# Token-major products for the convolution inputs of a one-layer hybrid decoder trunk, and later steps in every block-transpose turning

## The chip, the cores and the metric

The kernel runs on one core of one Trainium2 chip. The metric is the device time of one execution in microseconds (us). The core has five engines that run side by side and meet through semaphores: PE (TensorE, matrix products, with weight loads shown apart as PEld), DVE (VectorE), ACT (ScalarE), POOL (GpSimd) and SP (SyncE, which here only issues DMAs). ACT issues DMAs as well, out of the same in-order list as its arithmetic.

## The reference, cut to what matters

One layer with 256 tokens and a model width of 2048. The normed input is multiplied by one wide weight, whose columns are shared out among several branches:

```
proj = h @ w_in
(sb_q, sb_k, sb_v, sb_z, ssd_z, ssd_xbc, ssd_dt, mem_q, mem_z, gate_pre) = split(proj)
o_sb = stick_breaking_attention(sb_q, sb_k, sb_v) * silu(sb_z)          # 8 heads of 128
xbc  = silu(causal_depthwise_conv(ssd_xbc, conv_w, conv_b))             # 4096 channels, 4 taps
x_ssm, b_in, c_in = split(xbc)                                          # 2048, 1024, 1024
y    = ssd_chunked_scan(x_ssm, dt, a, b_in, c_in) + d_skip * x_ssm      # 8 groups of 4 heads
o_ssd = gated_group_rms_norm(y, ssd_z, ssd_norm_w)
o_mem = memory_cross_attention(mem_q, mem_n, w_mem_kv) * silu(mem_z)    # 4 heads of 256
g_sb, g_ssd, g_mem = split(sigmoid(gate_pre + b_gate))
merged = g_sb*(o_sb @ w_branch_sb) + g_ssd*(o_ssd @ w_branch_ssd) + g_mem*(o_mem @ w_branch_mem)
out = rms_norm(x + merged @ w_out, final_norm_w)
```

The change concerns `ssd_xbc`, the 4096 columns that go through the convolution along the tokens.

## The kernel before, in words

All products run on PE in a split float32 form. A weight piece of 512 KB arrives in `raw` (DMA issued by SP, 4 buffers), ACT copies it into a rounded high part `wh` (L146), DVE subtracts to get the low part `wl` (L150), 3 buffers each. The activations `hT` are held the same way, as high and low parts with the model dimension on the partitions.

There are two ways to multiply. `gemm` (L269 to L271) is token-major: 128 tokens of `hT` are the stationary operand and 512 weight columns stream past; for each of 16 k-tiles and both token halves it makes three products of 512 columns (high with high, high with low, low with high). A weight piece holds 2 k-tiles of 512 columns, so it feeds 12 products, and a product over the whole depth takes 8 pieces. `gemm_cols` (L229, L233) is channel-major: 128 weight columns are stationary, and high and low part of `hT` (2 x 256 columns) stream past, then the high part alone (256 columns) against the low weight. A piece there holds 4 k-tiles of 256 columns and feeds 8 products of 512 and 8 of 256 columns. Only the convolution uses `gemm_cols`: 8 groups of 512 channels, two calls each, 4 pieces a call, so 64 pieces in all, as many as 8 calls of `gemm` have.

The convolution needs channels on the partitions. `gemm_cols` delivers that at once: `fold` (L246 on ACT, L247 on DVE) adds the two halves of the accumulator into `cu`, and `taps` (L744, L747) makes four DVE operations for each tile of 128 channels, 32 tiles in all. Other products that need channels on the partitions use `turning`: DVE transposes 32 x 32 blocks out of the accumulator (L308), ACT issues a DMA that writes them to a scratch in DRAM (L313), later four DMAs that read them back in turned order (L322), and later still the result is used.

The order of the work is set by hand. Every weight piece ends with `pump()`, which advances a clock by one, runs what `defer(fn, n)` has put n pieces ahead, and advances one of two lanes of head-by-head work (memory heads, stick-breaking heads, then SSD groups). Everything is written into each engine's in-order list at that moment. Between the copy of one weight piece and that of the next, ACT therefore does whatever was due at that piece; a `wh` copy that comes late makes `wl` late on DVE and then the products late on PE.

After the convolution come the products of the merge gates and the branches. There each gate group has a sigmoid (L772), each SSD group exponentials of its decays `dec` (L812); these need different ACT tables, and a table load (ACT_TABLE_LOAD, L768 or L772) stands where they alternate. DVE adds a mask to the decays (L805), scales the inputs `xs` (L799), weighs the decays (L816) and adds the gate bias into `sig` (L907).

SiLU of the turned gate tiles `zT` and of the convolved tiles `cT` is done by `silu` (L203), four tiles at once. It is issued during the last four convolution groups and shortly after.

Of the kernel before, what the change touches and what calls it, by code (L numbers as in the profile page):

```python
# [10 lines left out]
F32 = mybir.dt.float32  # L11
F32R = mybir.dt.float32r
AF = mybir.ActivationFunctionType
# [3 lines left out]
P = 128  # L17
D = 2048
T = 256
NKT = D // P  # L20
GW = 512
# [4 lines left out]
LATE = 3  # L26
# [10 lines left out]
C_SSDZ, C_XBC, C_DT = 4096, 6144, 10240  # L37
# [4 lines left out]
def trunk_kernel(  # L42
# [6 lines left out]
    nc = tc.nc  # L49
# [4 lines left out]
    tmp = ctx.enter_context(tc.tile_pool(name="tmp", bufs=2))  # L54
# [7 lines left out]
    def nm(s):  # L62
        cnt[0] += 1
        return f"{s}_{cnt[0]}"
# [104 lines left out]
    late = []  # L169
    now = [0]  # L170

    def defer(fn, chunks=LATE):

        cnt[0] += 1
        heapq.heappush(late, (now[0] + chunks, cnt[0], fn))
# [26 lines left out]
    def silu(a, chunks=LATE):  # L202
        defer(lambda: nc.scalar.activation(a, a, AF.Silu), chunks)  # L203
# [35 lines left out]
    def fold(dst, acc):  # L239

        if isinstance(acc, list):
            for b in range(2):
                nc.scalar.activation(dst[:, b], acc[b][:, 1], AF.Copy)
                nc.vector.tensor_tensor(dst[:, b], acc[b][:, 0], dst[:, b], ALU.add)
        else:
            nc.scalar.activation(dst, acc[:, :, 1], AF.Copy)  # L246
            nc.vector.tensor_tensor(dst, acc[:, :, 0], dst, ALU.add)  # L247
# [53 lines left out]
    def turning(use=None, dst=None):  # L301

        scratch = dram.tile([2, P, 4, 4, 32], F32, name=nm("scratch"))

        def evac(rows):
            blocks = tmp.tile([P, 2, 4, 4, 32], F32, tag="blocks", name=nm("blocks"), bufs=1)
            for t in range(2):
                nc.vector.transpose(blocks[:, t].rearrange("p j k c -> p k j c"),  # L308
                                    rows[t].rearrange("p (k j c) -> p k j c", k=4, j=4))
            defer(lambda: away(blocks), 1)  # L310

        def away(blocks):
            nc.scalar.dma_start(scratch.rearrange("t p j k c -> p t (j k c)"),  # L313
                                blocks.rearrange("p t j k c -> p t (j k c)"))
            defer(back, 2)

        def back():
            cols = dst
            if dst is None:
                cols = tmp.tile([P, 8, P], F32, tag="turned", name=nm("turned"), bufs=1)  # L320
            for j in range(4):
                nc.scalar.dma_start(  # L322
                    cols[32 * j:32 * j + 32],
                    scratch[:, :, j].rearrange("t (i r) k c -> r (t i) (k c)", r=32))
            if use is not None:
                defer(lambda: use(cols), 3)
        return evac

    def quarter(a):
# [2 lines left out]
    def tiles(cols, k, n):  # L332
        return cols.rearrange("p i (k c) -> p k i c", c=32)[:, k:k + n]
# [19 lines left out]
    def blocked(a):  # L353
        return a.rearrange("p k (i c) -> p k i c", c=32)
# [47 lines left out]
    hT = Cols(NKT, "hT")  # L402
# [246 lines left out]

    for i, z in enumerate((zM, zS)):  # L650
        for q in range(2):
            silu(z[:, 4 * q:4 * q + 4], LATE + 5 + 2 * i + q)
    defer(start_mem, LATE + 9)

    qS = slot([P, 8, T], F32, "qS")
    kS = slot([P, 8, T], F32, "kS")
# [75 lines left out]

    cT = [slot([P, 8, T], F32, "cT") for _ in range(4)]

    def conv_evac(i0):
        def evac(acc):
            u = tmp.tile([P, 2, T], F32, tag="cu", name=nm("cu"), bufs=2)
            fold(u, acc)
            for b in range(2):
                defer(lambda b=b: taps(u[:, b], i0 + b), 1 + 2 * b)  # L740

        def taps(u, i):
            a = cT[i // 8][:, i % 8]
            nc.vector.tensor_scalar(a, u, convw[:, 3, i:i + 1], convb[:, i:i + 1], ALU.mult,  # L744
                                    ALU.add)
            for s in range(1, 4):
                nc.vector.scalar_tensor_tensor(a[:, s:T], u[:, 0:T - s],  # L747
                                               convw[:, 3 - s, i:i + 1], a[:, s:T],
                                               ALU.mult, ALU.add)
        return evac  # L750

    waiting = [zT[i // 2][:, 4 * (i % 2):4 * (i % 2) + 4] for i in range(4)]
    for i, g in enumerate((4, 5, 6, 7, 0, 1, 2, 3)):
        for j in range(2):
            gemm_cols(hT, NKT, w_in, C_XBC + g * GW + 2 * j * P, conv_evac(4 * g + 2 * j))
        waiting.append(cT[g // 2][:, 4 * (g % 2):4 * (g % 2) + 4])
        if i >= 4:
            for j in range(3):
                silu(waiting.pop(0), 6 if not waiting else 1 + j)


    oD = []
# [6 lines left out]
            tables[0] = True  # L769

    def sigmoid(a):
        nc.scalar.activation(a, a, AF.Sigmoid)  # L772
        tables[0] = False

# [2 lines left out]
    def ssd_group(g):  # L777

        heads = range(4 * g, 4 * g + 4)
        xT = [cT[i // 8][:, i % 8] for i in (2 * g, 2 * g + 1)]  # L780
        zg = turned(zT[g // 4], 2 * (g % 4), 2)

# [85 lines left out]
    def step_apart():  # L868
        yield
# [10 lines left out]

    def start_ssd():

        lanes[1].append(step_apart())
        for i in range(SSD_GROUPS):
            lanes[i % 2].append(ssd_group(i))
        for i in range(SSD_GROUPS):
            lanes[i % 2].append(ssd_cols(i))
# [127 lines left out]
    g = 3  # L1015
# [60 lines left out]
```

## Time and profile before

| what | value |
|---|---|
| median of 3 runs | 1217.72 us (1216.94 to 1218.15) |
| the profiled execution's own time | 1217.57 us |
| its span, first to last instruction | 1215.8 us |
| PE busy | 1204.7 us, 99% |
| DVE busy | 784.7 us, 65% |
| ACT busy | 636.1 us, 52% |
| POOL busy | 49.6 us, 4% |
| granted TensorE clock | 0.998 |
| convolution products, first to last | 469.9 to 658.4 us |
| first gate products and memory branch begin | 658.4 us |

A timeline row gives the start in us, the duration in us, the engine, the line, the operation, output and inputs, the shape and how many were merged into the row; in square brackets stands the idle time of the engine just before, and what ended it. "q" behind an engine's name marks its sequencer, which issues DMAs.

### The profile page before, as it was taken

Reading aid. Unit: us, or ns where it says so; the run is one execution under the profiler, and the core shown is the slowest. Engines: PE = TensorE matmul, PEld = TensorE weight load, DVE = VectorE, ACT = ScalarE, POOL = GpSimd, SP = SyncE. Lnnn points to the kernel's source line nnn. Section 1 sums busy time; section 2 is a strip of 40 time slices with the busy share of each in tenths; the row PEclk is TensorE's granted clock in tenths of the full one; section 3 lists DMA queues with packets and bytes.
Section 4 is the critical chain, followed back from the end, with each engine's and each line's share of the span. In section 5 each row is a group of like instructions: output and inputs, shape, how many; then the busy total and the mean of one; then the engine's idle time right before and its main releaser. Section 6 shows DMA issues by size and latency. Waiting matters only on the chain.

```text
span 1215.8 us, 15596 instructions
## 1 busy us (share of the span) xinstructions
PE 1204.7 (99%) x5852; PEld 1008.3 (83%) x5852; DVE 784.7 (65%) x995; ACT 636.1 (52%) x846; POOL 49.6 (4%) x50
## 2 busy tenths in 40 slices
PE   9999999999999999999999999999999999999997
PEld 7888888888888888888888888888888888888886
DVE  5685664556654555888878758677677755655752
ACT  6754543354445444545665756475756544434541
POOL 0000000000000000010100000000000010110101
PEclk9999999999999999999999999999999999999999
DMA  9978798786776778656567667676865677788751
GB/s 337 338 217 240 206 257 237 245 238 194 205 207 192 214 226 234 176 176 185 175 184 216 213 199 217 186 230 180 238 182 182 208 220 216 228 224 289 254 206 69
DMA packets 168091, 262.56 MB, mean 216 GB/s; under 512 B 11792, under 2 KB 65232, under 8 KB 167888
## 3 DMA queue, kind: packets, MB, share of 16 engines
q1 hardware_dynamic: 135456, 229.51, 62.5%
q10 hardware_dynamic: 32560, 32.06, 9.5%
q8 instruction: 45, 0.74, 0.3%
q14 instruction: 30, 0.25, 0.1%
HBM read 249.45 MB, written 12.09 MB: 215 GB/s over the span
## 4 chain that ended last, share of the span: by engine, by line
PE 93%; DMA 3%; ACT 1%; issue 1%; DVE 1%; ACTq 0%; SPq 0%; POOLq 0%; POOL 0%; DVEq 0%
PE acc L269 24%; PE acc L270 24%; PE acc L271 24%; PE acc L229 10%; PE acc L233 5%; DMA raw<-in_w_mem_kv_dram 1%; PE y L833 1%; DMA turned<-scratch 1%; DMA rows<-in_mem_dram 1%; DVE wl L150 1%; ACT wh L146 1%; PE acc L456 0%; PE acc L457 0%; PE dtp L517 0%; PE acc L1030 0%
## 5 line engine op out<-in xcount | busy, mean ns | idle before, releaser
L150 DVE TENSOR_TENSOR wl<-raw,wh 128x1024 fp32r<-128x1024 f32 (+1 forms) x409 | 502.7, 1233 | 320.0 <-ACT wh L146 318.0
L146 ACT ACTIVATE wh<-raw 128x1024 fp32r<-128x1024 f32 (+1 forms) x409 | 430.9, 1056 | 431.0 <-PE acc L271 311.2
L269 PE MATMUL acc<-wh,hT 128*128 128x512 f32 x896 | 351.5, 392 | 0.0
L270 PE MATMUL acc<-wl,hT 128*128 128x512 f32 x896 | 349.2, 390 | 0.2 <-DVE wl L150 0.2
L271 PE MATMUL acc<-wh,hT 128*128 128x512 f32 x896 | 349.0, 390 | 0.0
L271 PEld LDWEIGHTS acc<-wh,hT 128*128 128x128 f32 x896 | 168.2, 188 | 35.4
L270 PEld LDWEIGHTS acc<-wl,hT 128*128 128x128 f32 x896 | 168.3, 188 | 34.8 <-DVE wl L150 1.1
L269 PEld LDWEIGHTS acc<-wh,hT 128*128 128x128 f32 x896 | 168.3, 188 | 34.6 <-issue 0.5
L229 PE MATMUL acc<-hT,wh 128*128 128x512 f32 x512 | 161.5, 397 | 0.0
L233 PEld LDWEIGHTS acc<-hT,wl 128*128 128x128 f32 x512 | 96.2, 188 | 22.7
L233 PE MATMUL acc<-hT,wl 128*128 128x256 f32 x512 | 100.7, 278 | 0.0
L229 PEld LDWEIGHTS acc<-hT,wh 128*128 128x128 f32 x512 | 78.0, 189 | 0.1
L269 PE MATMUL acc<-wh,oD 128*128 128x512 f32 x128 | 49.8, 389 | 0.0
L270 PE MATMUL acc<-wl,oD 128*128 128x512 f32 x128 | 49.8, 389 | 0.0
L271 PE MATMUL acc<-wh,oD 128*128 128x512 f32 x128 | 49.8, 389 | 0.0
L747 DVE SCALAR_TENSOR_TENSOR cT<-cu,wcols,cT 128x255 f32<-128x255 f32 (+2 forms) x96 | 46.4, 483 | 3.4
L919 POOL TENSOR_TENSOR merged<-merged,sig 128x512 f32<-128x512 f32 x16 | 25.1, 1593 | 519.0 <-DVE sig L918 519.0
L269 PE MATMUL acc<-wh,mT 128*128 128x512 f32 x96 | 37.4, 390 | 0.0
L271 PE MATMUL acc<-wh,mT 128*128 128x512 f32 x96 | 37.4, 389 | 0.0
L270 PE MATMUL acc<-wl,mT 128*128 128x512 f32 x96 | 37.4, 389 | 0.0
L270 PEld LDWEIGHTS acc<-wl,oD 128*128 128x128 f32 x128 | 24.0, 188 | 5.0
L271 PEld LDWEIGHTS acc<-wh,oD 128*128 128x128 f32 x128 | 24.0, 188 | 5.0
(244 smaller groups left out, 1287.6 us busy)
## 6 DMA issues: line engine op xcount, KB each, us to landing
raw<-in_w_in_dram SPq DMA_DIRECT2D x288, 512.0 KB, 4.4
raw<-in_w_branch_ssd_dram SPq DMA_DIRECT2D x32, 512.0 KB, 4.4
raw<-in_w_mem_kv_dram SPq DMA_DIRECT2D x31, 512.0 KB, 6.0
raw<-in_w_out_dram SPq DMA_DIRECT2D x24, 512.0 KB, 5.7
scratch<-blocks ACTq DMA_DIRECT2D x19, 512.0 KB, 4.8
raw<-in_w_branch_mem_dram SPq DMA_DIRECT2D x16, 512.0 KB, 4.1
raw<-in_w_branch_sb_dram SPq DMA_DIRECT2D x16, 512.0 KB, 4.9
dec<-acT SPq DMA_DIRECT2D x24, 256.0 KB, 5.8
```

Of the source, the lines that this page charges most:

```text
L146: nc.scalar.activation(hi, src, AF.Copy, **({} if scale is None else {"scale": scale}))
L150: nc.vector.tensor_tensor(lo, src, h32, ALU.subtract)
L229: nc.tensor.matmul(halves[b], wh[:, kt - k0, b * P:(b + 1) * P], lhs.both(kt), start=first, stop=False, skip_group_check=True)
L233: nc.tensor.matmul(halves[b][:, 1], wl[:, kt - k0, b * P:(b + 1) * P], lhs.at(kt)[0], start=False, stop=last, skip_group_check=True)
L269: nc.tensor.matmul(a, lh[:, tt], wh[:, j], start=first, stop=False)
L270: nc.tensor.matmul(a, lh[:, tt], wl[:, j], start=False, stop=False)
L271: nc.tensor.matmul(a, ll[:, tt], wh[:, j], start=False, stop=last)
L747: nc.vector.scalar_tensor_tensor(a[:, s:T], u[:, 0:T - s], convw[:, 3 - s, i:i + 1], a[:, s:T], ALU.mult, ALU.add)
L833: nc.tensor.matmul(y[c:c + 64, b, t * P:(t + 1) * P], xs[:, s, 64 * e:64 * e + 64], dec[j][:, e], start=(j == 0), stop=(j == 2), skip_grou ...
L919: nc.gpsimd.tensor_tensor(merged[t][:, cs], merged[t][:, cs], sig[:, t], ALU.add)
```

## The change

The convolution's products are made by `gemm` as well, in 8 calls of 512 channels, and its result is turned by `turning`: two block transposes on DVE, one write and four reads through DRAM for each group, 8 groups. Two ACT copies then bring the turned tiles into `cu` (two buffers of two tiles), and the taps follow 1, 3, 5 and 7 pieces later. The SiLU of the groups 0 to 3 (the SSD inputs) is issued 8 pieces after the use by `conv_done`; if the SSD groups have started by then it waits until just before the next sigmoid. In all turnings, those of the other products included, the reads are issued 4 pieces after the write (2 before) and the use comes 4 pieces after the reads (3 before). The SiLU of `zM` and `zS` and the start of the memory heads move back by two pieces.

```diff
@@ turning
-            defer(back, 2)
+            defer(back, 4)
...
-                defer(lambda: use(cols), 3)
+                defer(lambda: use(cols), 4)
...
-            silu(z[:, 4 * q:4 * q + 4], LATE + 5 + 2 * i + q)
-    defer(start_mem, LATE + 9)
+            silu(z[:, 4 * q:4 * q + 4], LATE + 7 + 2 * i + q)
+    defer(start_mem, LATE + 11)
...
-    def conv_evac(i0):
-        def evac(acc):
-            u = tmp.tile([P, 2, T], F32, tag="cu", name=nm("cu"), bufs=2)
-            fold(u, acc)
-            for b in range(2):
-                defer(lambda b=b: taps(u[:, b], i0 + b), 1 + 2 * b)
+    def conv(i0):
+        def use(cols):
+            for k in (0, 2):
+                u = tmp.tile([P, 2, T], F32, tag="cu", name=nm("cu"), bufs=2)
+                nc.scalar.activation(blocked(u), tiles(cols, k, 2), AF.Copy)
+                for b in range(2):
+                    defer(lambda u=u, i=k + b: taps(u[:, i % 2], i0 + i), 1 + 2 * (k + b))
+            if i0 < 16:
+                defer(lambda: conv_done(i0 // 4), 8)
...
-        return evac
+        return turning(use)
+
+    silu_done = set()
+    exps = []
+
+    def conv_done(g, late=False):
+
+        if exps and not late:
+            waiting.append(g)
+            return
+        a = cT[g // 2][:, 4 * (g % 2):4 * (g % 2) + 4]
+        nc.scalar.activation(a, a, AF.Silu)
+        silu_done.add(g)
+
+    def silu_late():
+
+        while waiting:
+            conv_done(waiting.pop(0), True)
...
-        for j in range(2):
-            gemm_cols(hT, NKT, w_in, C_XBC + g * GW + 2 * j * P, conv_evac(4 * g + 2 * j))
-        waiting.append(cT[g // 2][:, 4 * (g % 2):4 * (g % 2) + 4])
-        if i >= 4:
-            for j in range(3):
-                silu(waiting.pop(0), 6 if not waiting else 1 + j)
+        gemm(hT, NKT, w_in, C_XBC + g * GW, conv(4 * g))
+        if g >= 4:
+            waiting.append(cT[g // 2][:, 4 * (g % 2):4 * (g % 2) + 4])
+        else:
+            for j in range(min(3, len(waiting))):
+                silu(waiting.pop(0), 1 + j)
...
     def sigmoid(a):
+        silu_late()
         nc.scalar.activation(a, a, AF.Sigmoid)
...
     def start_ssd():
 
+        exps.append(True)
```

Three places in the engines' lists matter below. The first is ACT at the start of the SSD groups, from the copy of one weight piece (the prediction calls it piece E) through the next (F) to the one after (G). Before, `sig` is the gate group and `dec` are decays of the second SSD group:

```order
L146 ACTIVATE wh_5819<-raw_5817 128x1024
L772 ACT_TABLE_LOAD
L772 ACTIVATE sig_5535<-sig_5535 128x1024
L904 DMA sig_5838<-in_b_gate_dram 128x512
L146 ACTIVATE wh_5843<-raw_5841 128x1024
L768 ACT_TABLE_LOAD
L812 ACTIVATE dec_5702<-dec_5702,nac 128x128 x2
L812 ACTIVATE dec_5704<-dec_5704,nac 128x128 x4
L146 ACTIVATE wh_5869<-raw_5867 128x1024
```

Now, at the same pieces (`wh_5597` is E, `wh_5626` F, `wh_5656` G; `cu` are the last convolution group's turned tiles, `cT_3780` the SiLU of the group before it):

```order
L146 ACTIVATE wh_5597<-raw_5595 128x1024
L739 ACTIVATE cu_5613<-turned_5499 128x512
L739 ACTIVATE cu_5615<-turned_5499 128x512
L764 ACT_TABLE_LOAD
L764 ACTIVATE cT_3780<-cT_3780 128x1024
L793 ACT_TABLE_LOAD
L793 ACTIVATE sig_5293<-sig_5293 128x1024
L927 DMA sig_5621<-in_b_gate_dram 128x512
L146 ACTIVATE wh_5626<-raw_5624 128x1024
L788 ACT_TABLE_LOAD
L834 ACTIVATE dec_5467<-dec_5467,nac 128x128 x2
L834 ACTIVATE dec_5469<-dec_5469,nac 128x128 x4
```

Two copies, a table load and a SiLU have come in between the copies of E and F. Four reads of a turning (L322) also stand now ahead of the table load three pieces earlier, in front of piece B.

The second place is DVE over the same stretch. Now, from the tap of one tile in front of piece C (`wl_5543`) through D (`wl_5568`) to the next tap, in front of E:

```order
L747 TENSOR_SCALAR cT_3780<-cu_5382,wcols 128x256
L750 SCALAR_TENSOR_TENSOR cT_3780<-cu_5382,wcols,cT_3780 128x255
L750 SCALAR_TENSOR_TENSOR cT_3780<-cu_5382,wcols,cT_3780 128x254
L750 SCALAR_TENSOR_TENSOR cT_3780<-cu_5382,wcols,cT_3780 128x253
L821 TENSOR_TENSOR xs_5534<-xp_5473,dts 128x512
L827 TENSOR_TENSOR dec_5467<-dec_5467,cmask 128x512
L827 TENSOR_TENSOR dec_5469<-dec_5469,cmask 128x512
L150 TENSOR_TENSOR wl_5543<-raw_5540,wh_5542 128x1024
L838 TENSOR_TENSOR dec_5386<-dec_5386,cbs_5441 128x512
L150 TENSOR_TENSOR wl_5568<-raw_5565,wh_5567 128x1024
L747 TENSOR_SCALAR cT_3780<-cu_5382,wcols 128x256
```

Before, the same rows stand there without the taps, which had all been done some pieces earlier. The last tap reads `cu_5382`, the buffer that the second copy ahead of F (`cu_5615`) overwrites.

The third place is ACT twelve pieces after F, at the sigmoid of the second gate group. Now:

```order
L764 ACT_TABLE_LOAD
L764 ACTIVATE cT_3780<-cT_3780 128x1024
L793 ACT_TABLE_LOAD
L793 ACTIVATE sig_5621<-sig_5621 128x1024
L788 ACT_TABLE_LOAD
L880 ACTIVATE xs_5439<-tot_5872,eps 128x256
L881 ACTIVATE xs_5439<-xs_5439 128x256
L882 ACTIVATE cbs_5441<-tot_5872,eps 128x256
L883 ACTIVATE xs_5439<-xs_5439 128x256
L927 DMA sig_5923<-in_b_gate_dram 128x512
L146 ACTIVATE wh_5928<-raw_5926 128x1024
```

Before, the first two rows, a table load and the SiLU of the last convolution group, are not there.

More of the change, by code (lines that the diff above doesn't have):

```diff
@@ L779, in ssd_group @@
         heads = range(4 * g, 4 * g + 4)
+        assert g // 2 in silu_done, g
         xT = [cT[i // 8][:, i % 8] for i in (2 * g, 2 * g + 1)]
```

## The prediction

> **What bounds the kernel now.** First the page's busy times, the chain that ended last, and the two largest groups off PE:
>
> ```profile
> PE 1204.7 (99%) x5852; PEld 1008.3 (83%) x5852; DVE 784.7 (65%) x995; ACT 636.1 (52%) x846; POOL 49.6 (4%) x50
> PE 93%; DMA 3%; ACT 1%; issue 1%; DVE 1%; ACTq 0%; SPq 0%; POOLq 0%; POOL 0%; DVEq 0%
> L150 DVE TENSOR_TENSOR wl<-raw,wh 128x1024 fp32r<-128x1024 f32 (+1 forms) x409 | 502.7, 1233 | 320.0 <-ACT wh L146 318.0
> L146 ACT ACTIVATE wh<-raw 128x1024 fp32r<-128x1024 f32 (+1 forms) x409 | 430.9, 1056 | 431.0 <-PE acc L271 311.2
> ```
>
> PE carries 93% of the chain. ACT's weight copies wait mostly for PE to free a buffer, DVE's low parts wait for ACT's copies. So two things alone can move the time: what PE's own products take, and places where ACT or DVE fall so far behind that a weight piece is late. What they do otherwise costs nothing.
>
> **The products.** In PE's timeline of the convolution, five pieces lie between these two rows, with nothing but their products in between:
>
> ```profile
> 572.30 0.63 PE L229 MATMUL acc<-hT,wh 128*128 128x512 f32 x2
> 586.23 0.63 PE L229 MATMUL acc<-hT,wh 128*128 128x512 f32 x2
> ```
>
> That is 13.93 us, 2.786 a piece. In the token-major products of the gates `zT`, with the same `hT`, these two starts lie 18 products apart:
>
> ```profile
> 419.81 0.39 PE L270 MATMUL acc<-wl,hT 128*128 128x512 f32 x1
> 423.89 0.39 PE L270 MATMUL acc<-wl,hT 128*128 128x512 f32 x1
> ```
>
> 4.08 us for 18 is 0.2267 a product, 2.72 for the 12 of a piece. Both ways stream the same number of columns; the channel-major form loses 0.066 us a piece. Over 64 pieces the change saves **4.2 us**, all of it on PE's path. The stick-breaking heads' products stay as they are.
>
> **What the convolution stage adds elsewhere.** For 512 channels, `fold` goes (two copies on ACT, two adds on DVE) and two block transposes and two copies come, each on a 128x512 tile as before. I cost that at nothing. New on ACT are five DMA issues per group, new on the DMA engines 1 MB per group. One of every eight pieces has the transposes and a tap together on DVE, and ACT waits for these transposes before it may issue the write. The fullest such piece on DVE, with a step of a stick-breaking head as well, is this one of before, whose low part PE wants at 599.06:
>
> ```profile
> 595.23 1.22 DVE L150 TENSOR_TENSOR wl<-raw,wh 128x1024 fp32r<-128x1024 f32 x1
> ```
>
> ```profile
> 599.06 0.39 PE L233 MATMUL acc<-hT,wl 128*128 128x256 f32 x2
> ```
>
> It is ready at 596.45, 2.6 us early; two transposes (1.3 us by the row at 282.97 below) leave half of that, and the following pieces have none. So I take 0; if that cover is gone it is some tenths at each of eight places.
>
> **The turnings that were there.** In the stage of `kT`, PE stood still once because ACT had waited for a turned tile; in the memory heads a piece of low weight had little to spare:
>
> ```profile
> 99.50 0.39 PE L269 MATMUL acc<-wh,hT 128*128 128x512 f32 x1
> 100.04 0.50 PE L270 MATMUL acc<-wl,hT 128*128 128x512 f32 x1 [0.15 <-DVE wl L150]
> ```
>
> ```profile
> 282.74 0.39 PE L270 MATMUL acc<-wl,hT 128*128 128x512 f32 x1
> ```
>
> ```profile
> 280.69 2.36 DVE L150 TENSOR_TENSOR wl<-raw,wh 128x1024 fp32r<-128x1024 f32 x2
> 282.97 1.31 DVE L308 STREAM_TRANSPOSE blocks<-acc 128x512 f32<-128x512 f32 x2
> ```
>
> The first gap is 0.54 instead of 0.23, and the next product adds a tenth: **0.4 us** that two and one more pieces of delay remove. The second: the first of two low parts ends at 281.92, 0.8 us before PE wants it at 282.74. Moved by two pieces, this head's step falls behind the transposes (1.31 us) of the next turning, so it comes about **0.5 us** late. The two cancel. SP's and POOL's lists keep their order.
>
> **The start of the SSD groups** is where I expect the loss. In the old list all taps are over before piece B. Now the last two groups are still being turned, and seven taps, two copies, two SiLUs and two table loads fall among the exponentials. What stands there now, on ACT, with pieces E, F and G being the copies at 685.72, 689.06 and 693.18 (A to D go before them):
>
> ```profile
> 658.62 0.60 ACT L246 ACTIVATE cu<-acc 128x512 f32<-128x512 f32 x1 [1.96 <-PE acc L233]
> 659.11 1.05 ACT L203 ACTIVATE cT<-cT 128x1024 f32<-128x1024 f32 x1
> ...
> 685.72 1.05 ACT L146 ACTIVATE wh<-raw 128x1024 fp32r<-128x1024 f32 x1
> ...
> 686.80 1.28 ACT L772 ACT_TABLE_LOAD   x1
> 688.09 1.06 ACT L772 ACTIVATE sig<-sig 128x1024 f32<-128x1024 f32 x1
> 689.06 1.04 ACT L146 ACTIVATE wh<-raw 128x1024 fp32r<-128x1024 f32 x1
> 690.12 1.28 ACT L768 ACT_TABLE_LOAD   x1
> 691.41 1.86 ACT L812 ACTIVATE dec<-dec,nac 128x128 f32<-128x128 f32 x6
> 693.18 1.99 ACT L146 ACTIVATE wh<-raw 128x1024 fp32r<-128x1024 f32 x2
> ```
>
> on DVE, with piece C's low part at 681.81:
>
> ```profile
> 655.04 0.41 DVE L744 TENSOR_SCALAR cT<-cu,wcols 128x256 f32<-128x256 f32 x1
> 655.49 1.52 DVE L747 SCALAR_TENSOR_TENSOR cT<-cu,wcols,cT 128x255 f32<-128x255 f32 x3
> ...
> 680.01 0.68 DVE L799 TENSOR_TENSOR xs<-xp,dts 128x512 f32<-128x512 f32 x1
> 680.61 1.28 DVE L805 TENSOR_TENSOR dec<-dec,cmask 128x512 f32<-128x512 f32 x2
> 681.81 1.22 DVE L150 TENSOR_TENSOR wl<-raw,wh 128x1024 fp32r<-128x1024 f32 x1
> 682.94 0.69 DVE L816 TENSOR_TENSOR dec<-dec,cbs 128x512 f32<-128x512 f32 x1
> ```
>
> the issue of four reads just behind a copy, and PE's first use of the low parts of F and G:
>
> ```profile
> 409.07 1.06 ACT L146 ACTIVATE wh<-raw 128x1024 fp32r<-128x1024 f32 x1 [1.66 <-PE acc L271]
> 409.10 1.81 ACTq L322 DMA_DIRECT2D zT<-scratch  x4
> ```
>
> ```profile
> 693.58 0.39 PE L270 MATMUL acc<-wl,hT 128*128 128x512 f32 x1
> ...
> 696.30 0.39 PE L270 MATMUL acc<-wl,hT 128*128 128x512 f32 x1
> ```
>
> F's low part is due 1.23 us after its copy, at 691.4, 2.2 us early; G's at 695.5, 0.8 us early. Now count from the time that PE would have without stalls.
>
> DVE: the four reads ahead of piece B end 0.8 us after a copy does (409.10 + 1.81 against 409.07 + 1.06), so everything in front of C starts at 680.8 instead of 680.0. Then a tap (0.41 + 1.52, 1.9), xs 0.6, two masks 1.2, low part C 1.15, one weighing 0.65, low part D 1.15, the next tap 1.9: 680.8 + 8.55 = 689.35.
>
> ACT: E's copy is over by 686.8. The first copy into `cu` runs at once, the second overwrites the buffer which that last tap reads and waits until 689.35. Queued behind it are the second copy (0.5 by the step from 658.62 to 659.11), a table load 1.3, the SiLU 1.0, another table load 1.3 and the sigmoid 1.0, so F's copy starts at 694.4 instead of 689.06. Its low part ends 2.3 us on, at 696.7: 3.1 us late. Behind F come the old table load 1.3 and the six decays 1.8; G's copy ends at 699.5, its low part at 700.8: **4.5 us late**, which contains F's 3.1. After G two pieces have no other work on ACT, and the lag is worked off. Bounds: were the tap over before 686.8, F would start at 692.1 and G would be 2.2 us late; were the raw pieces late as well (below), 1.7 us more. I take 4.5, since both lists are nearly without gaps from B to G.
>
> **Twelve pieces later** the second gate sigmoid comes in the same piece as the exponentials of the norm:
>
> ```profile
> 722.58 1.28 ACT L772 ACT_TABLE_LOAD   x1
> ...
> 727.74 2.00 ACT L146 ACTIVATE wh<-raw 128x1024 fp32r<-128x1024 f32 x2
> ```
>
> ```profile
> 729.72 0.39 PE L269 MATMUL acc<-wh,hT 128*128 128x512 f32 x1
> 730.10 0.50 PE L270 MATMUL acc<-wl,hT 128*128 128x512 f32 x1
> ```
>
> PE's step here is 0.38 instead of 0.23: the low part is 0.15 us late already, so nothing is to spare. A table load 1.28 and a SiLU of 1.0 more come in between: **2.2 us**, nearly all seen by PE.
>
> The row at 686.80 shows a table load of 1.28 us with ACT going on at 688.09, no wait around it. [...]
>
> **The sum** against the profiled execution's 1217.57: -4.2 - 0.4 + 0.5 + 4.5 + 2.2 = +2.6, 1220.2. The runs' median of 1217.72 lies 0.15 higher, so I predict **1220.3 us**. A measurement of this kernel can tell about 0.2%, 2.4 us, from no change; the forecast lies just above that.
>
> **The rivals.**
>
> One, not slower: the second copy into `cu` doesn't wait. If DVE's last tap ahead of E ends before 686.8 instead of at 689.35, which is the point that decides, the first place costs 2.2 instead of 4.5: +0.3 and 1218.0. For it speaks that my DVE sum starts from a piece delayed by reads whose issue may hide; against it that it needs 2.5 us from a list of 8.55.
>
> Two, faster: both places stay covered, and only PE's saving is left, -4.2 - 0.4 + 0.5 = -4.1, 1213.6. It needs a lead at G and at the second sigmoid which the rows (0.8 us early, 0.15 us late) don't show.
>
> Three, the transfers. By the stretches of the DMA view the engines are full just there:
>
> ```profile
> 660.00:665.00 5.00, 5.00 (x23) 4.13 (x22) 3.75 (x6) 2.50 (x4) 0.00 (x0) 1.00 0.88 287
> 665.00:670.00 5.00, 5.00 (x26) 4.16 (x25) 4.51 (x8) 2.85 (x3) 0.00 (x0) 1.00 1.00 187
> ```
>
> (the last two columns are the DMA share and GB/s). A write and four reads of 1 MB together come on top, some 3.5 us of all engines at 287 GB/s. If the pieces in front of B come 2 us later, the chain to G starts later and ends about 1.7 us later: 1222.0. [...] Against it: pieces lie buffered, and after 675 us the share falls.
>
> Four: the products don't get shorter, for a reason that the gates' rows don't show: 1220.3 + 4.2 = 1224.5.
>
> [...]
>
> **How the numbers follow.** Forecast 0.45, one 0.24, two 0.12, three 0.12, four 0.04, five 0.03. The forecast's own spread, 1218.5 to 1221.5, lies about six tenths above 1220.1 (0.2% over 1217.72): 0.27 of its 0.45. Slower: 0.27 + 0.12 + 0.04 + 0.03 = 0.46. Same: 0.18 + 0.24 = 0.42. Faster: 0.12. The range from 1214.5 to 1223.3 takes in the forecast, one, three and five; it leaves out four and most of two.
>
> **What would show it.** In the changed profile: pieces of the convolution at 2.72 us, with no idle ahead of their products; no wait at 99.5; at the start of the SSD groups a copy of `cu` that waits for a tap, then two table loads around a SiLU and late low parts with waits of PE of 4 to 5 us in sum; twelve pieces later a wait of PE of 2 us. I am wrong if PE has no waits at these two places, or if waits of PE appear inside the convolution, or if ACT's copies there wait for `raw`.

## The result, and the profile after

| | before | after |
|---|---|---|
| median | 1218.03 us (6 runs, 1216.94 to 1219.86) | 1225.11 us (6 runs, 1222.74 to 1228.43) |
| the profiled execution's own time | 1217.57 us | 1228.03 us |
| its span | 1215.8 us | 1226.1 us |

The changed kernel is slower: ratio 1.006, interval 1.005 to 1.007. The profiled execution of after lies 2.9 us above the median. The busy times, the chain that ended last, and the largest group of products with idle time ahead of it (3.5 us), from the page of after:

```profile
PE 1205.8 (98%) x5596; PEld 996.9 (81%) x5596; DVE 785.4 (64%) x995; ACT 640.9 (52%) x848; POOL 47.9 (4%) x50
PE 89%; DMA 4%; DVE 3%; ACT 3%; issue 1%; ACTq 0%; SPq 0%; POOLq 0%; POOL 0%; DVEq 0%
L270 PE MATMUL acc<-wl,hT 128*128 128x512 f32 x1152 | 450.2, 391 | 3.5 <-DVE wl L150 3.5
```

PE's share of the chain falls from 93% to 89%, and what takes its place is spread over DMA, DVE and ACT: late weight pieces, not more work (DVE is busy for 785.4 us where it was 784.7, ACT for 640.9 where it was 636.1).

To find the places, take the start of the first product of the same weight piece in both PE timelines, and subtract. Each number below is what a stretch lasts longer than in before (us); the columns e... are the experiments further down, all from their profiled executions.

| stretch, by the times of before | after | e2 | e11 | e9 | e10 | e7 | e4 | e5 | e8 |
|---|---|---|---|---|---|---|---|---|---|
| 0 to 145.4 (start-up) | 1.1 | 1.1 | -0.4 | -0.7 | -1.0 | 0.0 | 0.8 | -0.8 | 0.6 |
| 145.4 to 469.9 (memory heads) | 0.6 | 0.6 | 0.6 | 0.6 | 0.6 | 0.6 | 0.6 | 0.6 | 0.0 |
| 469.9 to 658.4 (convolution) | -3.5 | -3.5 | -3.5 | -3.2 | -3.4 | -2.8 | -1.7 | -2.4 | -3.9 |
| 658.4 to 682.5 (first gate group) | **1.4** | 0.0 | 0.0 | 1.4 | 0.0 | 1.5 | 1.5 | 0.0 | 0.0 |
| 682.5 to 700.4 (SSD groups start) | **6.5** | 4.7 | 2.8 | 4.5 | 3.7 | 6.8 | 0.0 | 0.0 | 0.0 |
| 727.0 to 739.6 (second sigmoid) | **4.0** | 2.4 | 4.0 | 4.0 | 1.0 | 1.0 | 0.0 | 0.0 | 0.0 |

Elsewhere the stretches agree within 0.3 us. In e9, e7 and e4 the convolution's row also holds a wait ahead of the first gate product (0.2, 0.6 and 0.8 us); it is absent wherever the row below shows 0.0. The start-up varies by 2 us between kernels that have the same instructions there (1.1 in after, -1.0 in e10), so its 1.1 us is no effect of the change.

**The products** became as short as forecast. PE's timeline of after, two starts 60 products (five pieces) apart:

```profile
568.55 0.39 PE L269 MATMUL acc<-wh,hT 128*128 128x512 f32 x1
...
582.15 0.39 PE L269 MATMUL acc<-wh,hT 128*128 128x512 f32 x1
```

13.60 us, 2.72 a piece, where before took 13.93. One piece later PE waits inside the convolution once:

```profile
585.55 0.39 PE L269 MATMUL acc<-wh,hT 128*128 128x512 f32 x1
586.11 0.50 PE L270 MATMUL acc<-wl,hT 128*128 128x512 f32 x1 [0.17 <-DVE wl L150]
```

0.56 instead of 0.23 us, and 0.1 on the next product: 0.44.

**The first gate group.** This is ACT's timeline of after where the first loss lies, and PE's:

```profile
648.65 1.06 ACT L146 ACTIVATE wh<-raw 128x1024 fp32r<-128x1024 f32 x1 [1.65 <-PE acc L271]
648.66 1.83 ACTq L322 DMA_DIRECT2D turned<-scratch  x4
654.93 0.36 ACTq L927 DMA_DIRECT2D sig<-in_b_gate_dram  x1
655.42 2.96 ACT L146 ACTIVATE wh<-raw 128x1024 fp32r<-128x1024 f32 x3 [5.70 <-DMA turned<-scratch]
```

```profile
656.62 0.41 PE L269 MATMUL acc<-wh,hT 128*128 128x512 f32 x1
657.80 0.50 PE L270 MATMUL acc<-wl,hT 128*128 128x512 f32 x1 [0.77 <-DVE wl L150]
```

ACT's sequencer has issued the four reads by 650.5, but issues the next entry of its list, the read of the gate's bias (L927), only at 654.93. The weight copies stand behind it: ACT idles 5.70 us, the profile gives the landing of the turned tile as what ended that, and then makes three copies in a row. PE gets its low part at 657.80 instead of 656.85. In the built order the bias read has two conditions, in before (first row) it had one:

```
L904 DMA sig_5535<-in_b_gate_dram 128x512 [waits Pool_49]
L927 DMA sig_5293<-in_b_gate_dram 128x512 [waits DMAHW0_49,Pool_49]
```

The added one is the semaphore that the first of the four reads just ahead of it raises when it has landed: the bias read goes out 6.3 us after that read was issued.

**The start of the SSD groups**, ACT's timeline of after (pieces F and G, as the prediction names them, are the copy at 695.78 and the first at 699.91; between the two lie a table load and six decays):

```profile
674.77 1.06 ACT L146 ACTIVATE wh<-raw 128x1024 fp32r<-128x1024 f32 x1 [3.11 <-DMA raw<-in_w_in_dram]
...
687.43 0.62 ACT L739 ACTIVATE cu<-turned 128x512 f32<-128x512 f32 x1
690.50 0.64 ACT L739 ACTIVATE cu<-turned 128x512 f32<-128x512 f32 x1 [2.46 <-DVE cT L750]
691.14 1.28 ACT L764 ACT_TABLE_LOAD   x1
692.44 1.06 ACT L764 ACTIVATE cT<-cT 128x1024 f32<-128x1024 f32 x1
693.52 1.28 ACT L793 ACT_TABLE_LOAD   x1
694.81 1.06 ACT L793 ACTIVATE sig<-sig 128x1024 f32<-128x1024 f32 x1
695.78 1.04 ACT L146 ACTIVATE wh<-raw 128x1024 fp32r<-128x1024 f32 x1
...
699.91 2.94 ACT L146 ACTIVATE wh<-raw 128x1024 fp32r<-128x1024 f32 x3
```

The forecast chain is there step by step: the second copy waits for a tap, then come two table loads around a SiLU. PE's waits on it:

```profile
684.83 0.39 PE L269 MATMUL acc<-wh,oM 128*128 128x512 f32 x1
686.90 0.50 PE L270 MATMUL acc<-wl,oM 128*128 128x512 f32 x1 [1.69 <-DVE wl L150]
...
696.87 0.51 PE L269 MATMUL acc<-wh,hT 128*128 128x512 f32 x1 [1.09 <-ACT wh L146]
```

The wait of 1.3 us ahead of 696.87 belongs to F's late copy, and 1.0 us for its low part follows; these are forecast. The one of 1.85 us behind 684.83 is not: it is piece C's low part, from a chain that began with the raw piece of 674.77.

**The second sigmoid**, PE's timeline of after, and one stretch of it (PE's busy time first, then after the five engines the granted clock and the DMA share):

```profile
735.59 0.39 PE L271 MATMUL acc<-wh,oM 128*128 128x512 f32 x1
737.31 0.50 PE L269 MATMUL acc<-wh,hT 128*128 128x512 f32 x1 [1.33 <-ACT wh L146]
738.57 0.78 PE L270 MATMUL acc<-wl,hT 128*128 128x512 f32 x1 [0.76 <-DVE wl L150]
739.15 0.63 PE L271 MATMUL acc<-wh,hT 128*128 128x512 f32 x1
739.57 0.63 PE L269 MATMUL acc<-wh,hT 128*128 128x512 f32 x1
```

```profile
740.00:745.00 5.00, 5.00 (x20) 4.09 (x19) 3.45 (x5) 1.74 (x5) 0.00 (x0) 0.80 1.01 214
```

Two waits of 1.5 and 1.0 us, and behind them products 0.43 us apart instead of 0.23, until 742: the granted clock, the share of full speed that PE is given (0.86 from 735 to 740 us, 0.80 in the row above), is at half for some 3.4 us.

### The profile page after: what moved, and what is told of

Same layout as the page of the kernel before. It is cut to its first block, busy times and chain, and to the rows that moved or that the text cites. A ratio compares the mean times of both kernels' runs of the same rounds, so it can differ in the third digit from the quotient of the medians.

```text
span 1226.1 us, 15163 instructions
## 1 busy us (share of the span) xinstructions
PE 1205.8 (98%) x5596; PEld 996.9 (81%) x5596; DVE 785.4 (64%) x995; ACT 640.9 (52%) x848; POOL 47.9 (4%) x50
## 4 chain that ended last, share of the span: by engine, by line
PE 89%; DMA 4%; DVE 3%; ACT 3%; issue 1%; ACTq 0%; SPq 0%; POOLq 0%; POOL 0%; DVEq 0%
PE acc L270 28%; PE acc L269 27%; PE acc L271 27%; DVE wl L150 2%; DMA raw<-in_w_mem_kv_dram 1%; PE y L855 1%; ACT wh L146 1%; DMA rows<-in_mem_dram 1%; DMA raw<-in_w_in_dram 1%; DMA rows<-in_x_dram 1%; DMA turned<-scratch 1%; DVE cT L750 0%; PE acc L456 0%; PE acc L457 0%; PE dtp L517 0%
## 5 line engine op out<-in xcount | busy, mean ns | idle before, releaser
L269 PE MATMUL acc<-wh,hT 128*128 128x512 f32 x1152 | 452.9, 393 | 2.5 <-ACT wh L146 2.4
L270 PE MATMUL acc<-wl,hT 128*128 128x512 f32 x1152 | 450.2, 391 | 3.5 <-DVE wl L150 3.5
L271 PE MATMUL acc<-wh,hT 128*128 128x512 f32 x1152 | 449.4, 390 | 0.0
L270 PEld LDWEIGHTS acc<-wl,hT 128*128 128x128 f32 x1152 | 216.8, 188 | 49.2 <-DVE wl L150 6.2
L269 PEld LDWEIGHTS acc<-wh,hT 128*128 128x128 f32 x1152 | 216.8, 188 | 48.1 <-ACT wh L146 4.0
L271 PEld LDWEIGHTS acc<-wh,hT 128*128 128x128 f32 x1152 | 216.7, 188 | 45.5
L308 DVE STREAM_TRANSPOSE blocks<-acc 128x512 f32<-128x512 f32 x48 | 31.4, 692 | 0.0
L269 PEld LDWEIGHTS acc<-wh,oD 128*128 128x128 f32 x128 | 24.0, 188 | 5.0
L271 PEld LDWEIGHTS acc<-wh,oD 128*128 128x128 f32 x128 | 24.0, 188 | 5.0
L270 PE MATMUL acc<-wl,oM 128*128 128x512 f32 x64 | 25.1, 393 | 2.0 <-DVE wl L150 2.0
L455 PE MATMUL acc<-wh,memT 128*128 128x512 f32 x64 | 25.1, 393 | 1.5 <-ACT memT L146 1.5
```

Source lines behind the costliest of these rows:

```text
L269: nc.tensor.matmul(a, lh[:, tt], wh[:, j], start=first, stop=False)
L270: nc.tensor.matmul(a, lh[:, tt], wl[:, j], start=False, stop=False)
L271: nc.tensor.matmul(a, ll[:, tt], wh[:, j], start=False, stop=last)
L455: nc.tensor.matmul(a, lh[:, tt], wh[:, g], start=first, stop=False)
```

## The experiments

The theory to test: three things make the loss, the bias read behind the reads of a turning, the late copies and SiLUs that the prediction named, and the half clock. The rivals: the added transfers by themselves (1 MB a group), the longer distances in all turnings, the table loads alone, or DVE's list. The kernel before, run beside each, had medians of 1218.0 to 1218.6 us.

**e1: the distances alone.** The kernel before with the edits of the distances and no other:

```diff
-            defer(back, 2)
+            defer(back, 4)
...
-                defer(lambda: use(cols), 3)
+                defer(lambda: use(cols), 4)
...
-            silu(z[:, 4 * q:4 * q + 4], LATE + 5 + 2 * i + q)
-    defer(start_mem, LATE + 9)
+            silu(z[:, 4 * q:4 * q + 4], LATE + 7 + 2 * i + q)
+    defer(start_mem, LATE + 11)
```

> The kernel before with only the later steps of the turnings (reads 4 pieces after the write, use 4 after the reads, the SiLU of zM and zS and the memory heads two pieces later); the convolution stays channel-major. If the loss sits in the lists of ACT and DVE at the start of the SSD groups, this changes next to nothing: minus 0.4 us at the first kT turning, plus 0.5 at the second head's transposes, so within 1 us of before (1218). If the delays themselves cost, because work of other stages comes later, it is 3 us or more slower, 1221 and above.

1219.07 us, ratio 1.0009 (1.0000 to 1.0018). Its profile has 0.55 us more in the stretch of the memory heads and 0.3 in all behind it. The distances are a small part.

**e6: the transfers alone.** The kernel before, with the DMAs of eight turnings of an idle tile put where after has them:

```diff
+    def idle_turning():
+        scratch = dram.tile([2, P, 4, 4, 32], F32, name=nm("scratch"))
+        nc.scalar.dma_start(scratch.rearrange("t p j k c -> p t (j k c)"),
+                            idle.rearrange("p t j k c -> p t (j k c)"))
...
+        defer(back, 4)
```

> The kernel before plus the transfers alone: for each of the 8 convolution groups a write of 512 KB to a scratch and four reads of 128 KB back, on ACT's list at the pieces where the change has them, of data that nobody uses. Products, taps and SiLUs stay as before. List theory: only the late weight pieces and the bias read queued behind four reads remain, 0 to 2.5 us at the start of the gate products; 1218 to 1220.5. Transfer theory: most of the loss that the changed kernel shows (7 us plus the 4 that its products save) is there, 1226 or more.

1217.97 us, ratio 1.0001 (0.9992 to 1.0010). In the median the transfers cost nothing that can be measured. ACT's timeline shows that the bias read waits here too:

```profile
655.20 0.36 ACTq L921 DMA_DIRECT2D sig<-in_b_gate_dram  x1
655.69 1.06 ACT L146 ACTIVATE wh<-raw 128x1024 fp32r<-128x1024 f32 x1 [4.68 <-DMA turned<-scratch]
```

ACT stops for 4.68 us instead of 5.70, and PE doesn't wait there; at the start of the SSD groups this profile has 1.5 us more than before. There the raw piece of the copy at 675.73 takes 9.8 us from issue to landing (8.1 in before), ACT waits 3.74 us for it, and a low part comes late on PE. So a slow transfer can cost about what the prediction's third rival said, here in an execution that lies 1.4 us above this kernel's median.

**e3: no late SiLU.** The changed kernel without the SiLUs of the convolution's groups 2 and 3, so a part of the computation is left out:

```diff
-        nc.scalar.activation(a, a, AF.Silu)
+        if not late:
+            nc.scalar.activation(a, a, AF.Silu)
```

> The changed kernel without the two late SiLUs (those of convolution groups 2 and 3 are left out, and with them the table load that each brings). List theory: at the first place F's copy loses a table load and a SiLU (2.3 us) but still waits for the tap, so about 2 us less of the 6.5 lost there; twelve pieces later the whole 2.2 to 4 us go, with the stretch at half clock. In all 4 to 6 us faster than the changed kernel, 1219 to 1221. Transfer theory: the DMAs are all still there, so it stays within 1.5 us of 1225.

1219.29 us, ratio 1.0015 (1.0006 to 1.0024). The second sigmoid's 4.0 us are gone altogether, without any half clock (the mean granted clock of this execution is 0.999), and the start of the SSD groups costs 3.9 instead of 6.5. The first gate group keeps its 1.4, and PE waits 1.0 us more ahead of its first product. The profiled execution is the longest of the 11, 2.9 us above their median.

**e4: the gates `zT` of groups 2 and 3 behind the convolution**, so that its taps and SiLUs are over before the SSD groups start; the SiLUs of these gates then wait for the third sigmoid:

```diff
-    for g in range(4):
+    for g in range(2):
         gemm(hT, NKT, w_in, C_SSDZ + g * GW, to_turned(zT[g // 2], g % 2))
...
+    for g in range(2, 4):
+        gemm(hT, NKT, w_in, C_SSDZ + g * GW, to_turned(zT[g // 2], g % 2))
```

> The changed kernel in another order: the last two groups of the gate z (8 pieces each) come after the convolution's products, so that the taps and the SiLUs of all convolution groups are over before the SSD groups' exponentials begin; the SiLUs are issued one a piece after the stick-breaking heads' last exponentials, those of the moved z groups at the third sigmoid. As many products and transfers as in the changed kernel, two table loads fewer. List theory: the saving of PE (4 us) stays and the losses of 6.5 and 4.0 go; left are the late weight pieces and the bias read, up to 2.5 us: 1214 to 1217, faster than before. Transfer theory: still two turnings at the same place, 1222 or more.

1218.10 us, ratio 0.9996 (0.9988 to 1.0005), less gain than expected. The two late places cost nothing now. What keeps it from the expected time is the bias read, 2.3 us (1.5 in the first gate group and 0.8 ahead of its first product), and a new wait of 0.98 us behind 526.86 in the convolution. DVE's timeline there:

```profile
522.44 1.11 DVE L747 TENSOR_SCALAR cT<-cu,wcols 128x256 f32<-128x256 f32 x1
523.59 1.52 DVE L750 SCALAR_TENSOR_TENSOR cT<-cu,wcols,cT 128x255 f32<-128x255 f32 x3
525.02 1.31 DVE L308 STREAM_TRANSPOSE blocks<-acc 128x512 f32<-128x512 f32 x2
...
526.69 1.21 DVE L150 TENSOR_TENSOR wl<-raw,wh 128x1024 fp32r<-128x1024 f32 x1
```

A tap, the next group's transposes and a step of a stick-breaking head stand between two low parts, and the second ends at 527.9 when PE wants it at 527.1.

**e2: the bias read later.** The changed kernel, with one edit:

```diff
-        nc.scalar.dma_start(sig[:, 0], b_gate[c0:c0 + GW].partition_broadcast(P))
+        defer(lambda: nc.scalar.dma_start(
+            sig[:, 0], b_gate[c0:c0 + GW].partition_broadcast(P)), 2)
```

> The changed kernel, with every gate group's bias read put two weight pieces later in ScalarE's list, so that the first no longer stands right behind the four reads of a turning. If the waits of 1.3 us at 656.62 and 660.42 us come from that read's place, they go. The time then falls by 1.3 us to about 1223.8 if nothing takes them back, and stays at 1225.1 if the last taps before the SSD groups set the end anyway, since TensorE then only arrives earlier at a wait whose end doesn't move. Rival: the raw pieces themselves are late there (the transfer engines are busy for 0.99 to 1.01 of that time): the waits stay, the ScalarE copies still end their wait on raw, 1225.1 us.

1222.84 us (5 runs, 1222.60 to 1224.03), ratio to before 1.0042 (1.0028 to 1.0055), 2.3 below after. ACT's timeline:

```profile
651.42 1.06 ACT L146 ACTIVATE wh<-raw 128x1024 fp32r<-128x1024 f32 x1 [1.66 <-PE acc L271]
...
655.04 0.36 ACTq L927 DMA_DIRECT2D sig<-in_b_gate_dram  x1
...
671.61 1.06 ACT L146 ACTIVATE wh<-raw 128x1024 fp32r<-128x1024 f32 x1 [1.33 <-PE acc L271]
```

The copies run through, and more than the 1.4 us goes: the copy that waited 3.11 us for its raw piece in after waits only for PE (671.61), and the start of the SSD groups falls from 6.5 to 4.7. This was in neither expectation. The bias read goes out at the same time as in after (655.04 and 654.93), so what has changed is not its transfer but ACT's stop. The stop delays the issue of that raw piece, which in after comes 15.9 us ahead of the first product of the SSD groups' stretch and in e2 17.3 us. Its transfer is longer in after as well, 8.5 us from issue to landing instead of 6.9 (8.3 in e3 and 8.4 in e9, where piece C is late by 1.6 and 1.8 us). In e7 below the issue is as late as in after, but the transfer takes 6.7 us, and ACT doesn't wait for that piece. So the 1.8 us came from the late issue and a slow transfer together.

**e7: the late SiLUs without table loads**, as a sigmoid right behind the gate's sigmoid and a multiplication on DVE:

```diff
-        nc.scalar.activation(a, a, AF.Silu)
+        if late:
+            s = t4([P, 4, T], "cs")
+            nc.scalar.activation(s, a, AF.Sigmoid)
+            nc.vector.tensor_tensor(a, a, s, ALU.mult)
+        else:
+            nc.scalar.activation(a, a, AF.Silu)
```

> The changed kernel, whose two late SiLUs are made as a sigmoid right behind the gate's sigmoid and a multiplication on VectorE, so that no function table is loaded for them. If the table loads are what makes the late SiLUs dear: 2.6 us of ScalarE's list gone at each of the two places, the second place without a wait (2.5 us) and so without the stretch at half clock (1.7 to 1.9 us), the first 2.4 us shorter: 1218.5 us, 1217.5 to 1221. Rival: at the first place the second copy of the turned columns, which waits for a tap, sets the end, and the table loads lie beside it: only the second place gains, 1220.9 us, 1220 to 1222. If the half clock doesn't come from the waits, it stays and 1.8 us with it.

1224.00 us, ratio 1.0047 (1.0034 to 1.0059): both expectations missed. The second sigmoid costs 1.0 instead of 4.0 us. At the start of the SSD groups the waits sum to 3.9 us, but 1.6 us of what is missing is piece C's wait, which is only 0.3 us here because its chain has no late raw piece. Ahead of F the edit adds a stop of its own, on DVE and ACT:

```profile
692.49 1.23 DVE L767 TENSOR_TENSOR cT<-cT,cs 128x1024 f32<-128x1024 f32 x1 [1.56 <-ACT cs L766]
```

```profile
693.75 0.36 ACTq L932 DMA_DIRECT2D sig<-in_b_gate_dram  x1
694.22 1.06 ACT L146 ACTIVATE wh<-raw 128x1024 fp32r<-128x1024 f32 x1 [1.76 <-PE acc L271]
```

The new tile `cs` shares its two buffers with the gate groups' `sig`, so the second bias read waits until the multiplication has read `cs` (to 693.72), and F's copy stands behind that read. So e7 doesn't take the table loads away alone. PE waits 1.7 us for F's copy and 1.0 us for its low part, and there the granted clock now falls (0.59 from 695 to 700 us, 0.72 from 700 to 705). PE's timeline of e7:

```profile
696.59 0.80 PE L270 MATMUL acc<-wl,hT 128*128 128x512 f32 x1 [0.76 <-DVE wl L150]
697.18 0.63 PE L271 MATMUL acc<-wh,hT 128*128 128x512 f32 x1
...
702.30 0.62 PE L271 MATMUL acc<-wh,hT 128*128 128x512 f32 x1
```

From 697.18 to 702.30 lie 12 steps of 0.427 us, 0.2 each over the usual, and with those at both ends, as an estimate from these rows, some 2.9 us of the 6.8 are clock.

**e9: four buffers for the copies.** The changed kernel, where the second copy now has no tap to wait for:

```diff
-                u = tmp.tile([P, 2, T], F32, tag="cu", name=nm("cu"), bufs=2)
+                u = tmp.tile([P, 2, T], F32, tag="cv", name=nm("cv"), bufs=4)
```

> The changed kernel with four buffers in place of two for the copies of the turned columns (with a tag of their own), so that the second copy of a pair no longer waits for the first pair's taps. If the second copy's wait at the start of the SSD groups is what makes the weight copies of pieces E, F and G late, the copy at 690.50 us starts about 3.3 us earlier, all behind it on ScalarE's list too, and TensorE's waits between 684 and 702 us fall from 6.3 to about 3 us: 1221.8 us, 1220.5 to 1223. Rival: the function tables and the late SiLU, or VectorE's list, set those ends by themselves: 1225.1 us, with waits of 6 us at that place.

1223.71 us, ratio 1.0050 (1.0037 to 1.0063). The place falls from 6.5 to 4.5 us, less than the expected 3.3 of gain. The 1.8 us wait for piece C stays; it goes with the bias read's move in e11.

**e11: e2 and e9 together.**

> The kernel e2 (bias reads two weight pieces later) with four buffers for the copies of the turned columns, the SiLUs as they are. In e2 TensorE's waits at the start of the SSD groups sum to 4.6 us, close to the 4.5 that the prediction gave to that place. If the second copy's wait for a tap, the step on which that 4.5 rested, holds about half of it (the prediction's own bound: 2.2 us without that wait), 2.2 to 2.6 us are left there: 1220.7 us, 1219.5 to 1222. Rival: VectorE's list (taps, weighings and low parts in one row) makes the low parts late by itself: 4.6 us stay, 1222.8 us.

1220.46 us, ratio 1.0024 (1.0015 to 1.0033), as expected. ACT's timeline at the start of the SSD groups:

```profile
683.39 1.14 ACT L739 ACTIVATE cv<-turned 128x512 f32<-128x512 f32 x2
684.55 1.28 ACT L764 ACT_TABLE_LOAD   x1
```

Both copies run back to back, no entry waits. The place costs 2.8 against 4.7 in e2: the second copy's wait is worth 1.9 us (2.0 between e9 and after), and the rest is the added work itself.

**e10: e2, e9 and e7 together.**

> The changed kernel with three edits at once: the bias reads two weight pieces later, four buffers for the copies, the two late SiLUs as sigmoids and multiplications. The order of the gates z and the convolution stays. If the loss consists of the bias read's place, the second copy's wait, the table loads and the half clock that follows such waits, some 1.0 us of waits stays at the start of the SSD groups and 1.1 at the second sigmoid, no half clock: 1217.3 us, 1216.3 to 1219. If VectorE's list (taps, added multiplications, steps of the groups in one place) is a bound of its own: 1220 us or more.

1219.58 us, ratio 1.0015 (1.0006 to 1.0024), between the two expectations (up to 1219, from 1220). The second sigmoid costs 1.0 us, but the start of the SSD groups 3.7, more than the 2.8 of e11. DVE's timeline:

```profile
688.64 1.23 DVE L767 TENSOR_TENSOR cT<-cT,cs 128x1024 f32<-128x1024 f32 x1 [0.94 <-ACT cs L766]
689.78 1.29 DVE L843 TENSOR_TENSOR dec<-dec,cbs 128x512 f32<-128x512 f32 x2
690.99 1.22 DVE L150 TENSOR_TENSOR wl<-raw,wh 128x1024 fp32r<-128x1024 f32 x1
```

The multiplication waits 0.94 us for ACT with the low part of 690.99 queued behind it, and DVE's list becomes the bound: the rival's mechanism shows, at a smaller price.

**e5: e4 and the later bias read.**

> The kernel e4 (gates z of groups 2 and 3 behind the convolution) with the bias reads two weight pieces later. There TensorE waited 2.2 us between 657 and 663 us and no wait followed that could take a gain back. If the bias read's place is the cause: 1216.0 us, 2.1 below e4. If the raw pieces are late by themselves: 1218.1 us as e4.

1215.60 us, ratio 0.9976 (0.9966 to 0.9985), faster than before; the wait at the first gate group is gone.

**e8: e5 with the distances restored.** The distances of 4 stay only between write and reads of the convolution's turnings, with 3 pieces to the use:

```diff
-    def turning(use=None, dst=None):
+    def turning(use=None, dst=None, gaps=(2, 3)):
...
-            defer(back, 4)
+            defer(back, gaps[0])
...
-                defer(lambda: use(cols), 4)
+                defer(lambda: use(cols), gaps[1])
...
-        return turning(use)
+        return turning(use, gaps=(4, 3))
...
-    defer(start_mem, LATE + 11)
+    defer(start_mem, LATE + 9)
```

> The kernel e5, with the four-piece distances only in the convolution's turnings and there 4 and 3 pieces, so that a tap no longer falls into the pieces in which the next group's transposes run; the other turnings have 2 and 3 pieces again and the memory heads start where they did before. If the waits left in e4 (0.55 us at the memory heads, 1.0 at 526.86, 0.4 at 586.22) are VectorE lists in which a tap, transposes and a head's step meet, they go: 1214.0 us, 1213.3 to 1215.5, below both kernels. Rival: what the products save is given back to the next bound whatever the order (the weight pieces' transfers): 1216 us or more, as e5.

1213.66 us (5 runs, 1213.05 to 1217.24), ratio 0.9968 (0.9956 to 0.9981): 4.9 us below the kernel before beside it, and the fastest of all. ACT's timeline at the bias read, four weight copies behind a turning's reads, where it no longer stops:

```profile
652.57 1.06 ACT L146 ACTIVATE wh<-raw 128x1024 fp32r<-128x1024 f32 x1 [1.66 <-PE acc L271]
652.58 0.36 ACTq L937 DMA_DIRECT2D sig<-in_b_gate_dram  x1
```

The convolution gains 3.9 us with no wait in it, and nothing is given back. So the token-major products are worth what they save on PE, if their follow-up work is over before the SSD groups start.

## Why the prediction was wrong

The sign and the forecast mechanism were right, the size was not: +2.6 us over the profiled execution were forecast, and the runs' median rose by 7.1. Two of the prediction's own signs of being wrong came: PE waits inside the convolution (0.44 us), and a copy ahead of the SSD groups waits for `raw` (3.11 us, at 674.77). Step by step:

- **Products, -4.2:** -3.9 where no wait disturbs them (e8), -3.5 in after with the wait of 0.44 at 585.55. The prediction looked at one piece of before as the fullest on DVE and took 0; the piece with a tap and two steps of a head was fuller, and two of its DVE operations were slow (last section).
- **The wait at 99.5, -0.4:** the wait is gone in after, but also in e6 and e8, which have the old distances there. It was one execution's accident in the profile of before, and no gain of the change.
- **Memory heads, +0.5:** 0.57 in after, 0.55 in e1, which has only the distances. Right.
- **Start of the SSD groups, +4.5:** 4.7 in e2, where nothing disturbs the place from ahead. PE is there 1.8 us earlier than in before (the sum of e2's stretches, start-up included), and F's copy stands at 692.64; put back by 1.8 that is 694.4, the forecast start. The waiting second copy was given 2.3 us (4.5 less the bound of 2.2) and measures 1.9. The bound is a little low: from 686.8 two copies, two table loads, the SiLU and the sigmoid put F at 692.4 and G 2.5 us late; e11, without that wait, has 2.8. Right in itself; in after the place costs 6.5.
- **Second sigmoid, +2.2:** 2.4 in e2. In after 4.0, with the half clock.
- **The step that failed** is the costing of the turnings' DMA issues in ACT's list. The prediction counted "the four reads ahead of piece B" at 0.8 us and, for the convolution, "five DMA issues per group" at nothing; it didn't look at what comes behind the reads ahead of the first gate group. There the bias read waits for the first of those reads to land, and all weight copies wait behind it: 1.4 us of PE at once, in each of the five profiles that have the changed convolution and the bias read at that place (after, e3, e4, e7, e9), and in none of the five where the read comes later (e2, e5, e8, e10, e11). In after 1.8 us more follow at the SSD groups (6.5 against 4.7, and 4.5 against 2.8 between e9 and e11), 3.2 in all; this second part also took a slow transfer, as e7 shows. Between medians the later read is worth 2.3 us from after to e2, 2.5 from e4 to e5, 3.3 from e9 to e11.
- **Rival three** had the late raw piece and about its 1.7 us, and put it down to busy transfer engines. That is half of it: the transfer was longer in after than in e2, and in e6's profile a transfer 1.7 us longer than in before costs 1.5 us. But the median of e6 is unchanged, and in e2 and e11, with all transfers still made, the wait is gone.
- **What no step had** is the half clock, 1.5 us in the profiled execution (4.0 against 2.4).

The sum with the measured terms, start-up left out: 0.6 - 3.5 + 1.4 + 6.5 + 4.0 = +9.0. Without the half clock it is 7.5, near the 7.1 of the medians; whether the executions without a profile had it is not known. In e2, without the failed step's cost, the terms sum to 4.2 and the median lies 4.3 above the kernel before beside it; the 1.6 us left over the forecast are the small terms above, the products' 0.7 and the 0.4 at 99.5 first. Rivals one, two and four fell (the copy did wait, neither place was covered, the products did get shorter). No run shows the dearer switch of tables that rival five's 0.03 stood for: in the rows of after above each table load takes 1.28 us and the next entry starts at once (692.44 behind 691.14, 694.81 behind 693.52).

## What to carry to other kernels

A faster product is only worth its gain if what hangs behind it still ends before the next stage needs the same in-order engines; here the order of two neighbouring products (the gates behind the convolution) decided between +7 and 0 us, and the place of one bias read and a few spacings gave 5 more. A DMA issue on a computing engine's list is an instruction that can wait (the bias read of after went out 4.4 us behind the issue of the four reads, and ACT idled 5.70 us): look in the built order at its conditions, and at what is queued behind it. When a wait looks new in one profile, check that it, or its absence, repeats in a second execution before booking it.

## What the runs showed of the hardware

**Half clock behind short waits.** Waits of 1.5 and 1.0 us, 0.2 us of products apart, were followed within about 1 us by products at 0.427 us in after, e9 and e11 at the second sigmoid, and not in e2, though e2 has the same two waits at the same place:

```profile
734.14 0.50 PE L269 MATMUL acc<-wh,hT 128*128 128x512 f32 x1 [1.33 <-ACT wh L146]
735.40 0.50 PE L270 MATMUL acc<-wl,hT 128*128 128x512 f32 x1 [0.76 <-DVE wl L150]
735.74 0.40 PE L271 MATMUL acc<-wh,hT 128*128 128x512 f32 x1
```

So the waits alone don't decide it. The traces hold the times at which the granted clock changes. In after it falls to half at 738.62 and is back at 742.04, in e9 at 736.05 and 739.47, in e11 at 732.50 and 735.91, in e7 at 695.95 and 702.78: 3.4 us each, in e7 6.8. In e2 it stays at 1.00 from 730 to 745 us. Behind the wait of 1.85 us that follows 684.83 in after it stays at 1.00 as well (from 685 to 705 us). What makes the difference was not shown; no experiment was made for it.

**DVE beside POOL.** In the convolution two DVE operations that overlap an operation of POOL take longer than the same operations elsewhere. POOL's timeline of after, and DVE's:

```profile
578.48 1.84 POOL L688 TENSOR_TENSOR lm<-lm,sp 128x384 f32<-128x384 f32 x1 [57.15 <-DVE sp L687]
580.90 1.84 POOL L688 TENSOR_TENSOR lm<-lm,sp 128x384 f32<-128x384 f32 x1 [0.58 <-DVE sp L687]
```

```profile
579.36 1.37 DVE L687 SCALAR_TENSOR_TENSOR sp<-lm,sp 128x384 f32<-128x384 f32 x1
...
581.79 1.11 DVE L747 TENSOR_SCALAR cT<-cu,wcols 128x256 f32<-128x256 f32 x1
```

L687 takes 0.55 us at 577.75 and 1.37 here, L747 0.41 and 1.11, and each ends 0.2 to 0.4 us behind the POOL operation that it overlaps; POOL's operation takes 1.84 us where a low part (578.22) had started ahead of it, and 1.01 at 517.58, where it started 0.03 us ahead of a low part, which then took 2.07 us instead of 1.22. Together the two DVE rows cost DVE's list 1.5 us, DVE has no idle time between them and the low part that PE waits for behind 585.55, and that one is 0.3 us late. In e4, too, both rows (1.37 us at 520.01 and 1.11 at 522.44) stand ahead of the wait behind 526.86. Why these operations take longer was not shown, and that taking POOL's work away would remove the wait was not tried.
